# Second layer of a hybrid trunk: first attention pair ahead of the value projection, ends of the recurrent branch behind the first two pairs

## The chip, the cores and the metric

The kernel runs on one core of a Trainium2 chip. The metric is the device time of one execution in microseconds (us). The engines are PE (TensorE), DVE (VectorE), ACT (ScalarE), POOL (GpSimd) and SP (SyncE, here only a queue for transfers). Each works through its own list of instructions in order and waits on semaphores for the others.

## The reference, cut to what matters

A two-layer decoder trunk on 512 tokens of width 1024, all in float32. The second layer's mixer is what the change touches. One input projection gives xr, gr, q, k and v (512 columns each). xr and gr feed a recurrent branch, q, k and v a stick-breaking attention with 8 heads of 64. Their outputs, side by side, go through one output projection.

```python
# recurrent branch C
xc = conv_b + sum(conv_w[j] * xpad[:, j:j + S] for j in range(4))     # causal, width 4
r = sigmoid(xc @ wa + ba); i = sigmoid(xc @ wx + bx)                  # 8 diagonal blocks of 64
log_a = -8 * r * softplus(-lam)
a = exp(log_a); u = sqrt(-expm1(2 * log_a)) * (i * xc)
h[t] = a[t] * h[t-1] + u[t]                                           # a scan over time
yc = h * gelu(gr)
# attention D, per head
z = (q @ k.T) / 8                                                     # masked: k before q
s = where(mask, log_sigmoid(-z), 0)
w = where(mask, exp(log_sigmoid(z) + (suffix sum of s over keys) - s), 0)
yd = w @ v
```

## The kernel before

All activations are kept transposed, 128 features by 512 tokens. Every float32 matrix product of a projection is done as three products of a high and a low part (`mm3`): a tile of weights arrives by DMA in `ws` (one of 2 buffers), ACT copies it into its high part `wh`, DVE subtracts to get the low part `wl` (5 buffers each), and PE runs 8 x 3 matmuls of 128 x 512 into one PSUM bank (`proj`, 24 matmuls). The projections' banks have the tag "g", 2 banks in turn, so a projection waits until the bank of the last but one has been emptied.

In `layer1` the second layer's mixer runs in this order:

- `griffin(xr)`, the recurrent branch, with 4 tiles of 128 channels. The four xr tiles already lie in PSUM. Per tile j, ACT copies xr out (`xp`), DVE does the convolution in four operations (`xc`), PE multiplies by the two gate matrices (`pa`, `px`), ACT takes two sigmoids (`r`, `ig`) and a tanh of `r`, DVE multiplies `ig` by `xc`. Then four projections of gr follow, each with a gelu on ACT (`gt`). Then the ends: per tile 4 Ln and Exp operations on ACT and 10 operations on DVE, one of them the scan, and the high and low parts of the result (`yh`, `yl`).
- `values(S_VD)`, the value projection: four weight tiles, 4 x 24 matmuls.
- four times `sb_pair`, attention for two heads: Q and K projections (`qk_pair`, which splits the results into high and low parts on ACT and DVE); five tiles of scores `z` by PE, for each a copy on ACT, a minimum on DVE, Exp and Ln on ACT, a maximum on DVE, and a high and low part (`sh` on ACT, `sl` on DVE); then PE forms the cumulative sums (`cu`, for the five tiles in two banks in turn, 6, 8 and 8 matmuls for the last three), DVE adds each to its `z`, ACT takes the Exp, and PE multiplies by the values (`po`). The output projection of the recurrent branch (`out_rows`) stands behind the fourth pair in the text.

The order of instructions on each engine is not written out. A scheduler makes it when the program is built, from the order of the text, priorities (weights are taken early, by `self.hp`) and the buffers: a tile of a pool has a tag, the tags have fixed numbers of buffers, and a tile gets a buffer when it is first written. `act` has 16 buffers of 128 x 512 and is used in the whole kernel; `z`, `l`, `sh` and `sl` (6, 4, 5 and 5) belong to the second layer's mixer. Before, `xp` was an `act` tile, and `r`, `ig` and `gt` took the attention's tags `z`, `sh` and `sl`. What the scheduler sets is fixed at build time: at run time an engine only waits.

Of the kernel before, what the change touches and what calls it, by code (L numbers as in the profile page):

```python
# [7 lines left out]
F32 = mybir.dt.float32  # L8
# [3 lines left out]
AF = mybir.ActivationFunctionType  # L12
ALU = mybir.AluOpType
AX = mybir.AxisListType

P = 128
T = 512
# [36 lines left out]
class Trunk:  # L54
# [631 lines left out]
    def griffin(self, xr):  # L686
        nc, cp = self.nc, self.cp
# [28 lines left out]
        st = []  # L716
        for j in range(4):
            ps = xr[j]
            xp = self.sb.tile([P, T], F32, tag="act", bufs=16, name=self.nm("xp"))
            nc.scalar.copy(xp, ps)  # L720
            xc = self.t2k("xc", tag="l")
            w = lambda t: par[:, C_CW + 4 * j + t:C_CW + 4 * j + t + 1]
            nc.vector.tensor_scalar(xc, xp, w(3), par[:, C_CB + j:C_CB + j + 1], ALU.mult, ALU.add)
            for t in (1, 2, 3):
                nc.vector.scalar_tensor_tensor(xc[:, t:T], xp[:, 0:T - t], w(3 - t), xc[:, t:T], ALU.mult, ALU.add)
            pa = self.bank("sc", "pa")
            nc.tensor.matmul(pa, gw[0][:, j, :], xc, start=True, stop=True)
            px = self.bank("ho", "px")
            nc.tensor.matmul(px, gw[1][:, j, :], xc, start=True, stop=True)
            r = self.t2k("r", tag="z")  # L730
            A(r, pa, AF.Sigmoid, bias=par[:, C_BA + j:C_BA + j + 1])
            ig = self.t2k("ig", tag="sh")
            A(ig, px, AF.Sigmoid, bias=par[:, C_BX + j:C_BX + j + 1])
            A(r, r, AF.Tanh, scale=sp4[:, j:j + 1])
            nc.vector.tensor_tensor(ig, ig, xc, ALU.mult)
            st.append((r, ig))
        gts = []
        for j in range(4):
            ps = self.proj(S_GR + j)
            g = self.t2k("gt", tag="sl")  # L740
            A(g, ps, AF.Gelu_apprx_tanh)
            gi = self.newest()
            gts.append(g)
        with self.tc.issue_after(gi):
            nc.scalar.preload_act_table_set("natural_log_exp_and_others")
            pre = self.newest()
        ys = []
        for j in range(4):
            t, ix = st[j]
            dn = self.t2k("dn", tag="l")  # L750
            nc.vector.tensor_scalar(dn, t, 0.5, 0.5, ALU.mult, ALU.add)
            w = self.t2k("w", tag="l")
            with self.tc.issue_after(pre):
                A(w, dn, AF.Ln)
            A(w, w, AF.Exp, scale=-1.0)
            nc.vector.tensor_tensor(dn, dn, w, ALU.mult)
            nc.vector.tensor_scalar(dn, dn, -1.0, 2.0, ALU.mult, ALU.add)
            nc.vector.tensor_tensor(w, w, dn, ALU.mult)
            nc.vector.tensor_scalar(t, t, 1e-19, None, ALU.max)
            with self.tc.issue_after(pre):  # L760
                A(t, t, AF.Ln)
            A(t, t, AF.Exp, scale=0.5)
            nc.vector.tensor_tensor(ix, ix, t, ALU.mult)
            nc.vector.tensor_tensor(ix, ix, w, ALU.mult)
            nc.vector.tensor_scalar(w, w, 1.0, None, ALU.subtract)
            nc.vector.tensor_tensor_scan(ix, w, ix, 0.0, ALU.mult, ALU.add)
            nc.vector.tensor_tensor(ix, ix, gts[j], ALU.mult)
            yh, yl = self.act("yh"), self.act("yl")
            self.put(ix, yh, yl)
            ys.append((yh, yl))  # L770
        return ys


    def sb_pair(self, hp, v):
        nc = self.nc
        A = nc.scalar.activation
        q, k = self.qk_pair(S_QD + hp, S_KD + hp, self.kz)
        yh, yl = self.act("yh"), self.act("yl")
        po = self.bank("ho", "po")
# [28 lines left out]
        for ti, parts in enumerate(tiles):  # L808
            z = sp[parts]
            ps = self.bank(("pt", "po")[ti % 2], "cu")  # L810
            lo = [(self.none, sp[e, i], o + (i - j) * P, T - i * P) for e, j, o in parts for i in range(j + 1, NTB)]
            mms = [(self.ntri, sp[parts[0][:2]][:2] + (0,), 0, T)] + lo
            for n, (w, (sh, sl, oi), c, m) in enumerate(mms):
                for x in (sh, sl):
                    nc.tensor.matmul(ps[:, c:c + m], w, x[:, oi:oi + m], start=n == 0 and x is sh,  # L815
                                     stop=n == len(mms) - 1 and x is sl)
            nc.vector.tensor_tensor(z, z, ps, ALU.add)
            A(z, z, AF.Exp)
            ex = self.newest()

        at = {(e, j): (sp[parts], o) for parts in tiles for e, j, o in parts}
        for j in range(NTB):
            for e in range(2):
                h = 2 * hp + e
# [8 lines left out]
    def layer1(self, xr):  # L833
# [14 lines left out]
        self.hp = 1  # L848
# [124 lines left out]
```

## Time and profile before

| | us |
|---|---|
| median of 3 runs | 1266.29 (1264.41 to 1266.33) |
| the profiled execution, its time | 1266.0 |
| the profiled execution, its span | 1264.2 |
| the four xr projections end, first gate projection begins | 690.0 |
| value projection, its matmuls | 720 to 742 |
| first attention pair, its scores begin | 757.9 |

A row of the trace in order of time reads: start, duration, engine, line, operation, what is written and from what, its size, how many were merged, and in brackets the idle time before it and who ended it. A row of windows reads: from:to, length, busy us of PE, PEld (weight load), DVE, ACT and POOL with the number of instructions, then the granted clock of PE, the share of the DMA engines and GB/s. A matmul's duration is longer than the step from one matmul to the next, since they overlap. Line numbers are those of the kernel before; `L247` to `L249` are the three products of `mm3`, `L236` and `L237` make `wh` and `wl`.

### The profile page before, as it was taken

Reading aid. Unit: us, or ns where it says so; the run is one execution under the profiler, and the core shown is the slowest. Engines: PE = TensorE matmul, PEld = TensorE weight load, DVE = VectorE, ACT = ScalarE, POOL = GpSimd, SP = SyncE. Lnnn points to the kernel's source line nnn. Section 1 sums busy time; section 2 is a strip of 40 time slices with the busy share of each in tenths; the row PEclk is TensorE's granted clock in tenths of the full one; section 3 lists DMA queues with packets and bytes.
Section 4 is the critical chain, followed back from the end, with each engine's and each line's share of the span. In section 5 each row is a group of like instructions: output and inputs, shape, how many; then the busy total and the mean of one; then the engine's idle time right before and its main releaser. Section 6 shows DMA issues by size and latency. Waiting matters only on the chain.

```text
span 1264.2 us, 15623 instructions
## 1 busy us (share of the span) xinstructions
PE 1244.6 (98%) x6311; PEld 1006.6 (80%) x6311; DVE 690.3 (55%) x1039; ACT 485.3 (38%) x748; POOL 28.9 (2%) x51
## 2 busy tenths in 40 slices
PE   9999999999999999999999999999999999999997
PEld 6787777779888888888889776777988888888885
DVE  7538788769334333334377596786733333433437
ACT  7446557442322222222233757673322222222120
POOL 2000000000000000000000000000000000000001
PEclk9999999999999999999999998999999999999999
DMA  6332111133232233332324221102423332333321
GB/s 237 117 112 63 61 51 51 51 117 103 98 99 90 96 99 100 100 94 91 99 91 143 67 86 48 48 20 84 151 67 100 100 98 87 99 101 100 100 67 67
DMA packets 34984, 115.46 MB, mean 91 GB/s; under 512 B 4176, under 2 KB 5200, under 8 KB 34912
## 3 DMA queue, kind: packets, MB, share of 16 engines
q1 hardware_dynamic: 33504, 112.77, 28.3%
q10 hardware_dynamic: 1152, 1.66, 0.4%
q8 instruction: 49, 0.80, 0.2%
q14 instruction: 23, 0.19, 0.0%
q0 software_dynamic: 256, 0.03, 0.0%
HBM read 112.32 MB, written 2.10 MB: 91 GB/s over the span
## 4 chain that ended last, share of the span: by engine, by line
PE 89%; DVE 6%; DMA 2%; ACT 2%; issue 1%; SPq 0%; DVEq 0%; ACTq 0%
PE pf L248 13%; PE pf L247 13%; PE pf L249 13%; PE po L249 8%; PE po L247 8%; PE po L248 8%; PE pj L247 5%; PE pj L248 5%; PE pj L249 4%; DMA ws<-in_wst 2%; PE sc L493 1%; PE po L660 1%; PE cu L815 1%; PE pv L248 1%; PE pv L247 1%; PE tr L317 1%
## 5 line engine op out<-in xcount | busy, mean ns | idle before, releaser
L236 ACT CAST wh<-ws 128x1024 fp32r<-128x1024 f32 x177 | 186.4, 1053 | 525.8 <-PE pf L248 190.5
L237 DVE TENSOR_TENSOR wl<-ws,wh 128x1024 fp32r<-128x1024 f32 x177 | 216.5, 1223 | 308.8 <-ACT wh L236 302.9
L247 PE MATMUL pf<-xh,wh 128*128 128x512 f32 x640 | 249.0, 389 | 0.0
L248 PE MATMUL pf<-xl,wh 128*128 128x512 f32 x640 | 249.0, 389 | 0.0
L249 PE MATMUL pf<-xh,wl 128*128 128x512 f32 x640 | 249.0, 389 | 0.0
L249 PEld LDWEIGHTS pf<-xh,wl 128*128 128x128 f32 x640 | 120.1, 188 | 25.1
L247 PEld LDWEIGHTS pf<-xh,wh 128*128 128x128 f32 x640 | 120.1, 188 | 24.9
L248 PEld LDWEIGHTS pf<-xl,wh 128*128 128x128 f32 x640 | 120.1, 188 | 24.7
L247 PE MATMUL po<-wh,hh 128*128 128x512 f32 x352 | 137.4, 390 | 0.0
L249 PE MATMUL po<-wh,hl 128*128 128x512 f32 x352 | 137.1, 390 | 0.1
L248 PE MATMUL po<-wl,hh 128*128 128x512 f32 x352 | 137.0, 389 | 0.0
L415 DVE TENSOR_TENSOR s<-s,pf 128x512 f32<-128x512 f32 x44 | 30.3, 688 | 141.8 <-PE pf L249 140.4
L247 PE MATMUL pj<-xh,wh 128*128 128x512 f32 x256 | 104.6, 410 | 1.7 <-DVE qk L595 1.1
L249 PE MATMUL pj<-xh,wl 128*128 128x512 f32 x256 | 105.4, 412 | 0.0
L248 PE MATMUL pj<-xl,wh 128*128 128x512 f32 x256 | 103.6, 405 | 0.0
L249 PEld LDWEIGHTS po<-wh,hl 128*128 128x128 f32 x352 | 66.0, 188 | 14.5 <-DVE hl L243 0.7
L247 PEld LDWEIGHTS po<-wh,hh 128*128 128x128 f32 x352 | 66.1, 188 | 14.3 <-DVE xt L328 0.6
L248 PEld LDWEIGHTS po<-wl,hh 128*128 128x128 f32 x352 | 66.1, 188 | 13.5
L247 PEld LDWEIGHTS pj<-xh,wh 128*128 128x128 f32 x256 | 48.4, 190 | 14.2 <-issue 4.6
L249 PEld LDWEIGHTS pj<-xh,wl 128*128 128x128 f32 x256 | 48.4, 189 | 10.6 <-issue 2.3
L248 PEld LDWEIGHTS pj<-xl,wh 128*128 128x128 f32 x256 | 48.4, 189 | 10.1 <-issue 1.4
L328 DVE TENSOR_TENSOR xt<-xt,po 128x512 f32<-128x512 f32 x64 | 43.4, 685 | 14.8 <-PE po L249 14.7
(242 smaller groups left out, 1818.7 us busy)
## 6 DMA issues: line engine op xcount, KB each, us to landing
ws<-in_wst SPq DMA_DIRECT2D x189, 512.0 KB, 3.5
gb<-in_lnp SPq DMA_DIRECT2D x8, 512.0 KB, 4.8
ws<-in_wst SPq DMA_DIRECT2D x12, 256.0 KB, 5.2
xt<-in_xT SPq DMA_DIRECT2D x8, 256.0 KB, 4.9
xt<-in_x SPq DMA_DIRECT2D x1, 2048.0 KB, 7.8
out_y<-xt SPq DMA_DIRECT2D x4, 256.0 KB, 2.0
out_y<-xt ACTq DMA_DIRECT2D x4, 256.0 KB, 2.0
gw<-in_gw ACTq DMA_DIRECT2D x2, 256.0 KB, 3.2
```

Source lines behind the costliest of these rows:

```text
L236: nc.scalar.copy(hi, st)
L237: nc.vector.tensor_tensor(lo, st, hi.bitcast(F32), ALU.subtract)
L247: mm(ps, ah, bh, start=first, stop=False)
L248: mm(ps, ah, bl, start=False, stop=False)
L249: mm(ps, al, bh, start=False, stop=last)
L317: nc.tensor.transpose(ps[:, j * P:(j + 1) * P], y[:, h * T + j * P:h * T + (j + 1) * P], self.ident)
L328: self.nc.vector.tensor_tensor(y, y, ps, ALU.add)
L415: nc.vector.tensor_tensor(s, s, pb, ALU.mult)
L493: nc.tensor.matmul(ps[u:u + 64, c * 64:(c + 1) * 64], E[:, c * P + u:c * P + u + 64], rhs, start=True, stop=True)
L660: nc.tensor.matmul(po[d, c], v[j][:, h * 64:h * 64 + 64], pT[:, t0 + j * P:t0 + (j + 1) * P], start=j == 0, stop=j == i)
L815: nc.tensor.matmul(ps[:, c:c + m], w, x[:, oi:oi + m], start=n == 0 and x is sh, stop=n == len(mms) - 1 and x is sl)
```

## The change

Three edits. `r`, `ig` and `gt` become `act` tiles. The ends of the recurrent branch leave `griffin` for a function of their own, `griffin_end(j)`, unchanged in what they compute; two of them are placed after the weights of the first pair, two after those of the second. `sb_pair` is cut in two, `sb_weights` (Q, K, scores, cumulative sums, Exp) and `sb_values` (the product with the values), and the value projection is placed between the two for the first pair. The numbers of buffers stay.

```diff
-            r = self.t2k("r", tag="z")
+            r = self.sb.tile([P, T], F32, tag="act", bufs=16, name=self.nm("r"))
             A(r, pa, AF.Sigmoid, bias=par[:, C_BA + j:C_BA + j + 1])
-            ig = self.t2k("ig", tag="sh")
+            ig = self.sb.tile([P, T], F32, tag="act", bufs=16, name=self.nm("ig"))
             A(ig, px, AF.Sigmoid, bias=par[:, C_BX + j:C_BX + j + 1])
...
-            g = self.t2k("gt", tag="sl")
+            g = self.sb.tile([P, T], F32, tag="act", bufs=16, name=self.nm("gt"))
             A(g, ps, AF.Gelu_apprx_tanh)
...
-        ys = []
-        for j in range(4):
-            t, ix = st[j]
-            dn = self.t2k("dn", tag="l")
...
+        self.gr = [(r, ig, g) for (r, ig), g in zip(st, gts)]
+        self.pre = pre
+
+    def griffin_end(self, j):
+        nc = self.nc
+        A = nc.scalar.activation
+        t, ix, gt = self.gr[j]
+        dn = self.t2k("dn", tag="l")
...
-        yc = self.griffin(xr)
+        self.griffin(xr)
         self.hp = 600
-        v = self.values(S_VD)
-        self.hp = 600
-        yd = []
+        yc, yd = [], []
         for hp in range(4):
-            yd.append(self.sb_pair(hp, v))
+            at = self.sb_weights(hp)
+            if hp == 0:
+                v = self.values(S_VD)
+            if hp < 2:
+                yc += [self.griffin_end(2 * hp + i) for i in range(2)]
+            yd.append(self.sb_values(hp, v, *at))
             if hp == 3:
                 self.out_rows(yc, S_WO1)
```

How the instructions now stand, at the three places that the prediction speaks of. The first is ACT in the recurrent branch, from just after the copy of the first xr tile (`xp_5547`). `xp_5564`, `xp_5581` and `xp_5598` are the copies of the second to fourth xr tile, `r` and `ig` the two sigmoids (the second `r` of a tile is its tanh), `wh` a weight tile's high part. Before:

```order
L720 COPY xp_5564<-pj_5309 128x512
L720 COPY xp_5581<-pj_5310 128x512
L715 DMA gw_5543<-in_gw 128x512
L715 DMA gw_5544<-in_gw 128x512
L720 COPY xp_5598<-pj_5311 128x512
L731 ACT_TABLE_LOAD
L731 ACTIVATE r_5558<-pa_5554,par 128x512
L236 CAST wh_5840<-ws_5838 128x1024
L733 ACTIVATE ig_5560<-px_5556,par 128x512
L734 ACTIVATE r_5558<-r_5558,sp_65 128x512
L731 ACTIVATE r_5575<-pa_5571,par 128x512
L733 ACTIVATE ig_5577<-px_5573,par 128x512
```

Now:

```order
L715 DMA gw_5543<-in_gw 128x512
L715 DMA gw_5544<-in_gw 128x512
L731 ACT_TABLE_LOAD
L731 ACTIVATE r_5558<-pa_5554,par 128x512
L733 ACTIVATE ig_5560<-px_5556,par 128x512
L734 ACTIVATE r_5558<-r_5558,sp_65 128x512
L236 CAST wh_5789<-ws_5787 128x1024
L720 COPY xp_5564<-pj_5309 128x512
L731 ACTIVATE r_5575<-pa_5571,par 128x512
L734 ACTIVATE r_5575<-r_5575,sp_65 128x512
L733 ACTIVATE ig_5577<-px_5573,par 128x512
L720 COPY xp_5581<-pj_5310 128x512
```

The copy of tile j+1 now stands behind both sigmoids of tile j, where all four copies stood ahead of the first sigmoid; the weight tile ahead of the second copy is that of the first K projection, where it was one of the value projection.

The second place is PE at the end of the second gr projection (`pj_5654`) and the beginning of the third (`pj_5687`), with the gate products of tiles 2 and 3 (`pa_5588`, `px_5590`, `pa_5605`, `px_5607`):

```order
+L247 MATMUL pj_5654<-xh,wh_5650 128x512
+L248 MATMUL pj_5654<-xl,wh_5650 128x512
+L249 MATMUL pj_5654<-xh,wl_5651 128x512
+L727 MATMUL pa_5588<-xc_5583,gw_5543 128x512
+L729 MATMUL px_5590<-xc_5583,gw_5544 128x512
+L727 MATMUL pa_5605<-xc_5600,gw_5543 128x512
+L729 MATMUL px_5607<-xc_5600,gw_5544 128x512
 L247 MATMUL pj_5687<-xh,wh_5683 128x512
 L248 MATMUL pj_5687<-xl,wh_5683 128x512
```

The gate products of the last two tiles now stand together behind the whole second gr projection, with no projection's matmul between them; before, those of tile 2 stood after that projection's seventh matmul, those of tile 3 after its twenty-first, with fourteen matmuls between.

The third place is DVE in the second attention pair, where it adds the cumulative sums to the scores (`z` from `cu`), as PE's sums come. Before (`l` with `z` is the maximum, `sl` a low part, `qk` a part of the third pair's Q):

```order
L801 TENSOR_TENSOR l_6335<-l_6335,z_6334 128x512
L817 TENSOR_TENSOR z_6263<-z_6263,cu_6349 128x512
L817 TENSOR_TENSOR z_6281<-z_6281,cu_6358 128x512
L804 TENSOR_TENSOR sl_6346<-l_6335,sh_6345 128x512
L595 SCALAR_TENSOR_TENSOR qk_6409<-pj_6418,qk_6409 64x512
L817 TENSOR_TENSOR z_6299<-z_6299,cu_6367 128x512
L817 TENSOR_TENSOR z_6319<-z_6319,cu_6376 128x512
L817 TENSOR_TENSOR z_6334<-z_6334,cu_6387 128x512
```

Now (`dn`, `w`, `r` and `ig` are the recurrent ends of tiles 2 and 3; ahead of this piece stand a `wl` and two maxima):

```order
L819 TENSOR_TENSOR z_6220<-z_6220,cu_6306 128x512
L806 TENSOR_TENSOR sl_6288<-l_6277,sh_6287 128x512
L806 TENSOR_TENSOR sl_6303<-l_6292,sh_6302 128x512
L819 TENSOR_TENSOR z_6238<-z_6238,cu_6315 128x512
L819 TENSOR_TENSOR z_6256<-z_6256,cu_6324 128x512
L760 TENSOR_TENSOR dn_6355<-dn_6355,w_6357 128x512
L767 TENSOR_TENSOR ig_5594<-ig_5594,r_5592 128x512
L819 TENSOR_TENSOR z_6276<-z_6276,cu_6333 128x512
L761 TENSOR_SCALAR dn_6355<-dn_6355 128x512
L755 TENSOR_SCALAR dn_6375<-r_5609 128x512
L762 TENSOR_TENSOR w_6357<-w_6357,dn_6355 128x512
L819 TENSOR_TENSOR z_6291<-z_6291,cu_6344 128x512
```

The recurrent ends of tiles 2 and 3 now stand among the additions, and the last part of the third pair's Q, which frees the bank for the fourth pair's, has moved from ahead of the third addition to behind eight operations that follow the fifth.

More of the change, by code (lines that the diff above doesn't have):

```diff
@@ L746, in griffin @@
             pre = self.newest()
-        ys = []
-        for j in range(4):
-            t, ix = st[j]
-            dn = self.t2k("dn", tag="l")
[L751 to L770, printed above, removed]
@@ L775, in sb_pair, with sb_weights @@
+    def sb_weights(self, hp):
         nc = self.nc
@@ L777, in sb_pair @@
         q, k = self.qk_pair(S_QD + hp, S_KD + hp, self.kz)
-        yh, yl = self.act("yh"), self.act("yl")
-        po = self.bank("ho", "po")
         tiles = (((0, 3, 384), (0, 1, 0)), ((1, 3, 384), (1, 1, 0)), ((0, 2, 0), (1, 2, 256)), ((0, 0, 0),), ((1, 0, 0),))
@@ L819, in sb_pair, with sb_values @@
             ex = self.newest()
-        at = {(e, j): (sp[parts], o) for parts in tiles for e, j, o in parts}
+        return {(e, j): (sp[parts], o) for parts in tiles for e, j, o in parts}, ex
+    def sb_values(self, hp, v, at, ex):
+        nc = self.nc
+        yh, yl = self.act("yh"), self.act("yl")
+        po = self.bank("ho", "po")
         for j in range(NTB):
```

22 lines of the change are left out of this document (20 added, 2 removed).

## The prediction, made before the result was known

> **What bounds the kernel now.** I read the page first, then PE's rows in order of time from 676 to 870 us (the second layer's mixer), then ACT's and DVE's rows of the same stretch.
>
> ```profile
> PE 1244.6 (98%) x6311; PEld 1006.6 (80%) x6311; DVE 690.3 (55%) x1039; ACT 485.3 (38%) x748; POOL 28.9 (2%) x51
> ...
> PE 89%; DVE 6%; DMA 2%; ACT 2%; issue 1%; SPq 0%; DVEq 0%; ACTq 0%
> ```
>
> PE sets the end. The change leaves every matmul in place, so its worth is the difference in the time PE waits, or runs at a low clock. The first attention pair is the worst place of before:
>
> ```profile
> 753.69 0.47 PE L247 MATMUL pj<-xh,wh 128*128 128x512 f32 x1 [1.06 <-DVE qk L595]
> 757.90 0.33 PE L793 MATMUL z<-qk,qk 128*128 128x128 f32 x1 [1.02 <-DVE qk L600]
> 772.47 0.28 PE L815 MATMUL cu<-sl,none 128*128 128x128 f32 x1
> 775.13 0.80 PE L815 MATMUL cu<-sh,ntri 128*128 128x512 f32 x1 [2.39 <-DVE z L817]
> 781.49 0.28 PE L793 MATMUL z<-qk,qk 128*128 128x128 f32 x1
> ...
> 774.00:775.00 1.00, 0.00 (x0) 0.00 (x0) 1.00 (x2) 1.00 (x3) 0.00 (x0) 0.64 0.80 106
> 775.00:776.00 1.00, 0.87 (x2) 0.78 (x3) 1.00 (x3) 1.00 (x2) 0.00 (x0) 0.50 0.92 356
> 780.00:781.00 1.00, 1.00 (x4) 0.90 (x3) 0.96 (x2) 0.60 (x1) 0.00 (x0) 0.50 0.00 0
> 781.00:782.00 1.00, 1.00 (x10) 0.90 (x9) 0.31 (x1) 0.61 (x2) 0.00 (x0) 0.94 0.00 0
> ```
>
> Waits of 1.06, 1.02 and 2.39 us; and after the last one the granted clock (the last number but two in a window's row) is 0.50 until about 781.1, six us after PE had work again.
>
> **Gain in the first pair.** Its cumulative sums (6+8+8 matmuls) took 775.13 to 781.49, 6.36 us, at half clock. The second pair's same 22 took 4.02 us with a wait of 0.32 inside:
>
> ```profile
> 800.30 0.50 PE L815 MATMUL cu<-sh,ntri 128*128 128x512 f32 x1 [0.26 <-DVE z L817]
> 803.02 0.47 PE L815 MATMUL cu<-sh,ntri 128*128 128x512 f32 x1 [0.32 <-DVE z L817]
> 804.32 0.45 PE L247 MATMUL pj<-xh,wh 128*128 128x512 f32 x1
> ```
>
> So the low clock cost 6.36 - (4.02 - 0.32) = 2.7 us. With the waits that is 1.06 + 1.02 + 2.39 + 2.7 = 7.2, and about 0.4 for PE's restarts. The pair now has two blocks of the value projection as filler (48 matmuls, as many as the Q and K projections gave it), no recurrent end on DVE ahead of its K parts, and no weight tile among its exps: I leave it 0.4 us of waits. **-7.2 us.** Moving the projection's four weight transfers behind two others on SP's queue costs nothing: they have some 40 us before their use.
>
> **Loss in the recurrent branch.** The order in which ACT now stands (shown above) puts the copy xp of tile j+1 behind both sigmoids of tile j. The durations of that chain:
>
> ```profile
> 690.02 0.40 PE L247 MATMUL pj<-xh,wh 128*128 128x512 f32 x1
> 694.36 0.39 PE L248 MATMUL pj<-xl,wh 128*128 128x512 f32 x1
> 695.33 1.10 PE L727 MATMUL pa<-xc,gw 128*128 128x512 f32 x2 [0.59 <-PE pj L248]
> 698.52 1.02 PE L727 MATMUL pa<-xc,gw 128*128 128x512 f32 x2
> 699.62 0.40 PE L247 MATMUL pj<-xh,wh 128*128 128x512 f32 x1
> ...
> 690.22 0.82 ACTq L715 DMA_DIRECT2D gw<-in_gw  x2
> 696.47 0.69 ACT L731 ACTIVATE r<-pa,par 128x512 f32<-128x512 f32 x1 [3.50 <-PE pa L727]
> 698.03 1.05 ACT L236 CAST wh<-ws 128x1024 fp32r<-128x1024 f32 x1 [0.87 <-PE pj L248]
> 698.98 0.68 ACT L733 ACTIVATE ig<-px,par 128x512 f32<-128x512 f32 x1
> 699.57 0.71 ACT L734 ACTIVATE r<-r,sp 128x512 f32<-128x512 f32 x1
> 700.18 0.67 ACT L731 ACTIVATE r<-pa,par 128x512 f32<-128x512 f32 x1
> 710.54 1.28 ACT L741 ACT_TABLE_LOAD   x1
> 711.83 0.60 ACT L741 ACTIVATE gt<-pj 128x512 f32<-128x512 f32 x1
> ...
> DMA to landing us min/median/max: 2.8/3.2/3.7
> L723 DVE TENSOR_SCALAR xc<-xp,par x4: 535/680/898, 690.3 to 696.3; 128x512 f32<-128x512 f32 x4
> L725 DVE SCALAR_TENSOR_TENSOR xc<-xp,par,xc x12: 731/739/743, 691.9 to 701.8; 128x511 f32<-128x511 f32 x4, 128x510 f32<-128x510 f32 x4, 128x509 f32<-128x509 f32 x4
> 700.03 1.22 DVE L237 TENSOR_TENSOR wl<-ws,wh 128x1024 fp32r<-128x1024 f32 x1
> 701.16 0.68 DVE L735 TENSOR_TENSOR ig<-ig,xc 128x512 f32<-128x512 f32 x1
> ```
>
> A projection's matmul takes (694.36 - 690.02)/19 = 0.228 us, a gate product 699.62 - 698.52 - 0.23 = 0.87. On ACT a sigmoid or tanh takes 0.6 (0.7 where the next reads it), a wh 0.95; on DVE a convolution 0.6 + 3 x 0.74, a wl 1.15. Walked through in before's times:
>
> - *Tile 0.* Convolution and gw's landing at 693.4; pa and px to 695.3 (wait 0.6, as now). The first gate projection's last 11 matmuls end at 697.8.
> - *Tile 1.* ACT ends tile 0's tanh at 696.7 and meets wh, whose buffer is still read by that projection's 23rd matmul; as at 698.03 above, it waits, until 697.75. Behind it stands xp1, 698.7 to 699.3. The second gate projection needs the bank that xp1 empties: **wait 1.6.** It starts at 699.4. DVE does wl, then the convolution, to 702.9; 16 matmuls end at 703.0, no wait. pa, px and 8 matmuls end at 706.6.
> - *Tile 2.* r 704.1, tanh to 705.4, ig to 706.1, xp2 to 706.7; DVE multiplies ig, starts the convolution, does a wl in its middle, ends at 710.8. **Wait 4.2**, and PE has nothing else in its order.
> - *Tile 3.* After 4.2 idle us the clock is at half, as after 2.39 above. pa and px take 3.5 and end at 714.3; tanh, ig to 715.0, xp3 to 715.6, convolution to 718.6: **wait 4.3.** pa, px to 722.1.
> - *Gelu.* The third gate projection needs the bank of the first, emptied by a gelu that is now behind ig3 and a table load: 722.2 + 0.6 + 1.3 + 0.6 = 724.8, **wait 2.65.**
>
> The waits sum to 12.75, four gate products at half clock add 4 x 0.87 = 3.5, and tile 0 is unchanged: 16.2. Six us of half clock at the third projection, as after 775, lose another 3.0: **+19.2 us.** At full clock throughout it would be 1.6 + 4.2 + 4.8 + 2.9 = 13.5 (the third wait grows, since px ends earlier than r's chain). ACT saves two of five table loads here, 2.6 us, while it waits.
>
> **Loss in the second pair.** It now takes the filler and the neighbours that the first pair had: Q and K of the next pair, two weight tiles on ACT and DVE, and two recurrent ends instead of one.
>
> ```profile
> 773.19 1.29 DVE L801 TENSOR_TENSOR l<-l,z 128x512 f32<-128x512 f32 x2
> 774.39 0.68 DVE L817 TENSOR_TENSOR z<-z,cu 128x512 f32<-128x512 f32 x1
> 805.40 2.90 PE L826 MATMUL po<-z,v 128*64 128x512 f32 x16
> L818 ACT ACTIVATE z<-z x20: 621/631/634, 775.4 to 853.9; 128x512 f32<-128x512 f32 x20
> L766 DVE TENSOR_TENSOR_SCAN ig<-w,ig 128x512 f32<-128x512 f32 x4 | 4.9, 1223 | 0.1
> L757 DVE TENSOR_SCALAR dn<-dn 128x512 f32<-128x512 f32 x4 | 1.7, 422 | 0.0
> ```
>
> The wait of 2.39 came from a wl and two maxima ahead of the first addition; the same three stand there now. Its K parts are not late by the 1.02, so I bound it by 1.4 and 2.4 and take 1.9. Count on from the first addition's start. Two sl precede the second addition, which ends at 4 x 0.6 = 2.4 (two additions or maxima take 1.2 in the rows above); PE's first group of six (3.7 - 2 x 1.3 = 1.1 us, a group of eight being 804.32 - 803.02) ends at 0.6 + 1.1: it waits 0.8, and ends its two groups of eight at 5.1. DVE ends the third addition at 3.1; before the fifth stand five operations of the recurrent ends and the fourth addition, four of two inputs at 0.6 and two of one input at 0.34, 3.1 in all; addition and exp end at 3.1 + 3.1 + 0.7 + 0.7 = 7.6. po needs that exp and has no projection in front of it any more: 2.5. After po (2.9) the fourth Q projection waits for the last part of the third's Q, behind eight operations with a scan, about 5.3 us after the fifth addition: 1.75. Sum 6.95, less before's 0.26 + 0.32: **+6.4.** Whether the clock drops is open: the 2.5 exceeds the 2.39 that dropped it, but a slow po would run in time that PE waits anyhow. Between 0 and 2.7 I take 1.3: **+1.3.** The third and fourth pairs keep their order; between -2 and +2, taken as 0.
>
> **Sum.** 19.2 - 7.2 + 6.4 + 1.3 = +19.7, of which I take 19, since the branch's warm-up may be shorter. The profiled execution took 1266.0 us (span 1264.2 and 1.8 around it; the runs' median is 1266.29): **1285 us**.
>
> [...]
>
> **Rivals.**
> - *The waits are too short for the clock to matter* (chance 0.22): the branch costs 13.5 (never at half) to 16.2 (at half only between its waits), the second pair no clock: with -7.2 + 6.4 that is 1279 to 1281. For it: only one drop in 190 us of this stage. Against: 4.2 us idle is nearly twice the wait that dropped it.
> - *The second pair does not inherit* (0.15): ACT is faster than I think, the additions come in time: 19 - 6.4 - 1.3, so 1277. For it: the later pairs of before wait 0.3 at a time with similar neighbours.
> - *Both pairs of idle stretches halve the clock, the third pair is late too* (0.1): 1288 to 1292.
> - *Not slower* (0.05): the four waits of the branch vanish under the gate projections as they do now, where PE's rows between 690 and 708.9 show 0.6 us of waiting. Then -7.2 + 6.4 + 1.3, about 1266; it decides if the branch's waits stay under 3 us. Against it stands PE's order: between px2 and pa3 it has no other instruction, so a 3 us convolution is bare.
>
> **How the numbers follow.** The forecast has 0.48. The range takes in the second rival and part of the third: 1275 to 1291. A change under 0.2% (2.5 us) can't be told from none. Slower: 0.95; same 0.03, faster 0.02.
>
> **What would show it.** PE's rows around pa and px: waits of 1.6, 4.2, 4.3 and 2.7 us on DVE xc and ACT gt, a granted clock of 0.5 for some 15 us there, no wait over 1 us in the first pair, and in the second a wait over 1 us on DVE z ahead of its sums, of over 2 us ahead of po. If PE's waits at pa are under 1 us each, the walk is wrong, and the time falls to 1266 or below.

## The result, and the profile after

| | before | changed |
|---|---|---|
| median, us | 1266.19 | 1285.30 (1284.92 to 1286.24) |
| span of the profiled execution, us | 1264.2 | 1283.0 |
| ratio of the times, 95% interval | | 1.0154 (1.0138 to 1.0171) |

The changed kernel is 1.5% slower: 1285.3 us, where 1285.0 was forecast. Both medians are of four runs. The page of its profile answers to the one shown of before as follows (busy time by engine):

```profile
PE 1249.4 (97%) x6311; PEld 1005.8 (78%) x6311; DVE 690.3 (54%) x1039; ACT 482.3 (38%) x746; POOL 28.9 (2%) x51
```

The same number of matmuls keeps PE busy 4.8 us longer, while the span grew by 18.8: 14 us are idle time of PE, and most of the rest are matmuls at a low clock (PE was busy for 17.10 us at 0.50, in the three stretches whose windows stand below, and for 9.40 before, 3.41 from 245.22 and 5.99 from 774.29; half of the difference is 3.85 of the 4.8 us). Most of both stands in one place, the recurrent branch. These are PE's rows of the changed kernel in order of time there: its first instruction, its waits of over half a microsecond, the last of them ahead of the third gate projection (row 724.56), and a row of the fourth pair that is used further down.

```profile
688.91 0.40 PE L247 MATMUL pj<-xh,wh 128*128 128x512 f32 x1
...
698.43 0.50 PE L247 MATMUL pj<-xh,wh 128*128 128x512 f32 x1 [1.39 <-ACT xp L720]
709.96 2.05 PE L727 MATMUL pa<-xc,gw 128*128 128x512 f32 x2 [4.05 <-DVE xc L725]
718.12 2.04 PE L727 MATMUL pa<-xc,gw 128*128 128x512 f32 x2 [4.41 <-DVE xc L725]
724.56 0.50 PE L247 MATMUL pj<-xh,wh 128*128 128x512 f32 x1 [2.69 <-ACT gt L741]
...
869.18 0.47 PE L817 MATMUL cu<-sh,ntri 128*128 128x512 f32 x1 [0.16 <-DVE z L819]
```

From the first gate projection to the third, before took 690.02 to 708.92, 18.9 us; now it is 688.91 to 724.56, 35.65. Windows of the changed kernel over the same stretch, cut where the granted clock (the last number but two) changes:

```profile
708.82:722.47 13.65, 7.50 (x8) 2.35 (x8) 4.36 (x7) 4.54 (x7) 0.00 (x0) 0.50 0.13 40
...
725.88:729.29 3.41, 3.41 (x10) 2.67 (x9) 0.00 (x0) 0.00 (x0) 0.00 (x0) 0.50 0.00 0
```

PE has 7.50 us of work in the 13.65 us at half clock: the engines that it waits for (DVE 4.36, ACT 4.54) are not busy all the time either. It is a chain of single steps, each waiting for the one before.

ACT's rows show why. The copies `xp` of the second and third tile stand at 697.80 and 705.17, each behind the sigmoids of the tile ahead, which wait for PE (2.43 and 4.87):

```profile
693.68 0.69 ACT L731 ACTIVATE r<-pa,par 128x512 f32<-128x512 f32 x1 [2.43 <-PE pa L727]
...
697.80 0.58 ACT L720 COPY xp<-pj 128x512 f32<-128x512 f32 x1
703.25 0.69 ACT L731 ACTIVATE r<-pa,par 128x512 f32<-128x512 f32 x1 [4.87 <-PE pa L727]
...
705.17 0.57 ACT L720 COPY xp<-pj 128x512 f32<-128x512 f32 x1
```

The attention pairs: in the first pair the longest wait in PE's rows is now 0.16 us (at 766.59) and the clock stays at 1.00. These are the second pair's waits of over half a microsecond.

```profile
813.78 0.50 PE L817 MATMUL cu<-sh,ntri 128*128 128x512 f32 x1 [2.38 <-DVE z L819]
815.67 0.77 PE L817 MATMUL cu<-sh,ntri 128*128 128x512 f32 x1 [0.64 <-ACT r L766]
826.63 0.50 PE L247 MATMUL pj<-xh,wh 128*128 128x512 f32 x1 [2.22 <-DVE qk L595]
```

Windows of the same kernel, up to the fall of the clock and as long as it is low:

```profile
811.40:814.63 3.23, 0.85 (x6) 0.77 (x6) 3.23 (x6) 3.23 (x7) 0.00 (x0) 1.00 0.51 133
814.63:821.46 6.83, 6.19 (x21) 4.88 (x20) 5.48 (x11) 5.23 (x10) 0.00 (x0) 0.50 0.04 15
```

The waits and the low clock that left the first pair have come back in the second. Where PE waits 2.38 us at 813.78, DVE and ACT are busy without a pause (3.23 of 3.23 us). DVE's rows of that time show what stands ahead of the first addition to a `z`: a `wl` and two maxima (`l`).

```profile
810.70 1.23 DVE L237 TENSOR_TENSOR wl<-ws,wh 128x1024 fp32r<-128x1024 f32 x1 [0.25 <-ACT wh L236]
811.84 1.29 DVE L803 TENSOR_TENSOR l<-l,z 128x512 f32<-128x512 f32 x2
813.04 0.68 DVE L819 TENSOR_TENSOR z<-z,cu 128x512 f32<-128x512 f32 x1
```

### The profile page after: what moved, and what is told of

It is laid out like the page before. It is cut to its first block, busy times and chain, and to the rows that moved or that the text cites. A ratio compares the mean times of both kernels' runs of the same rounds, so it can differ in the third digit from the quotient of the medians.

```text
span 1283.0 us, 15623 instructions
## 1 busy us (share of the span) xinstructions
PE 1249.4 (97%) x6311; PEld 1005.8 (78%) x6311; DVE 690.3 (54%) x1039; ACT 482.3 (38%) x746; POOL 28.9 (2%) x51
## 4 chain that ended last, share of the span: by engine, by line
PE 89%; DVE 6%; ACT 3%; DMA 1%; issue 1%; SPq 0%; DVEq 0%; ACTq 0%
PE pf L248 12%; PE pf L247 12%; PE pf L249 12%; PE po L249 8%; PE po L247 8%; PE po L248 8%; PE pj L247 5%; PE pj L248 5%; PE pj L249 5%; PE sc L493 1%; PE pv L247 1%; PE pv L248 1%; PE pv L249 1%; PE po L660 1%; DMA ws<-in_wst 1%; PE tr L317 1%
```

## The experiments

Two theories were to be told apart. Mine: the recurrent branch pays nearly all of the loss, because `r`, `ig` and `gt` now take buffers from the same row as the copies `xp`. The rival: the new places of the value projection and of the recurrent ends pay it. Beyond that I wanted to know how much of the branch's loss is the low clock, what delays the second pair, and if a version of the change is worth having. Each kernel was compared with the kernel before on the same chip; the last column is (ratio - 1) x 1265 us, so it can differ by some tenths from a difference of medians. The intervals are about 1 to 2.6 us wide to each side.

| kernel | median, us | ratio to before, 95% | us over before |
|---|---|---|---|
| the change | 1285.3 | 1.0154 (1.0138 to 1.0171) | +19.5 |
| copies first | 1267.7 | 1.0021 (1.0012 to 1.0031) | +2.7 |
| tiles only | 1283.9 | 1.0144 (1.0127 to 1.0161) | +18.2 |
| copies from other buffers | 1269.1 | 1.0029 (1.0019 to 1.0039) | +3.7 |
| gaps kept busy | 1280.7 | 1.0119 (1.0104 to 1.0135) | +15.1 |
| values only | 1282.6 | 1.0141 (1.0127 to 1.0155) | +17.8 |
| all ends in the first pair | 1283.8 | 1.0139 (1.0118 to 1.0159) | +17.6 |
| copies first, all ends in the first pair | 1263.2 | 0.9981 (0.9972 to 0.9990) | -2.4 |
| copies first, ends 2 / 0 / 2 | 1269.6 | 1.0034 (1.0021 to 1.0048) | +4.3 |
| copies first, ends 2 / 1 / 1 | 1265.3 | 0.9998 (0.9988 to 1.0007) | -0.3 |
| the same, weights later | 1261.8 | 0.9976 (0.9967 to 0.9985) | -3.0 |
| the same, weights midway | 1265.2 | 0.9999 (0.9990 to 1.0008) | -0.1 |

### The copies first

```diff
-        st = []
-        for j in range(4):
-            ps = xr[j]
+        xps = []
+        for ps in xr:
             xp = self.sb.tile([P, T], F32, tag="act", bufs=16, name=self.nm("xp"))
             nc.scalar.copy(xp, ps)
+            xps.append(xp)
+        st = []
+        for j in range(4):
+            xp = xps[j]
```

> The changed kernel, with the four copies xp taken in a loop of their own ahead of the branch's loop over tiles, so that they get their buffers among the activations before any r or ig does. Nothing else differs. Theory (the shared buffers serialise the branch): the waits of 1.39, 4.05, 4.41 and 2.69 us and the half clock between them go, the branch takes 18.9 us again from the first gate projection to the third where it took 35.7, and the second pair stays as it is: about 1285.3 - 17 = 1268. Rival (most of the loss comes from the value projection's new place): at most 4 us are won, 1281 or more. Between them, 1272 to 1276, would mean that the waits went but the copies or r and ig bring a new one.

16.8 us of the 19.5 are gone. One window over the branch of this kernel:

```profile
688.20:707.20 19.00, 18.41 (x67) 11.93 (x66) 14.20 (x21) 12.52 (x18) 1.22 (x2) 1.00 0.19 56
```

PE is busy 18.41 of 19.0 us at a clock of 1.00: there is no room for a wait of more than the 0.6 that stood there before. The value projection and the ends are where the change put them, so they do not pay the 16.8. What is left, +2.7, is the balance of the first pair's gain and of what the later pairs lose. In this trace they lose more than in the change: their low clock lasts 6.82 us from 793.31, 3.42 from 806.97 and 3.42 from 827.45, where the pairs of the change have 6.83 in all. So the branch alone costs more than 16.8, by the rows of the change 16.75 up to the third gate projection and 1.7 of half clock behind it.

### The tiles only

In the kernel before, with the rest of it untouched:

```diff
-            r = self.t2k("r", tag="z")
+            r = self.sb.tile([P, T], F32, tag="act", bufs=16, name=self.nm("r"))
...
-            ig = self.t2k("ig", tag="sh")
+            ig = self.sb.tile([P, T], F32, tag="act", bufs=16, name=self.nm("ig"))
...
-            g = self.t2k("gt", tag="sl")
+            g = self.sb.tile([P, T], F32, tag="act", bufs=16, name=self.nm("gt"))
```

> The kernel before, with only r, ig and gt taken from the activations' buffers; the value projection, and the recurrent branch in one piece, stay where they were. Theory: the branch pays its whole loss here too, 1266.2 + 17 = 1283, with waits of about 1.4, 4, 4.4 and 2.7 us ahead of the gate products and the third gate projection. Rival (the wait needs the new places, too): 1266, with 0.6 us of waiting in the branch as before. Everything behind 745 us should look as before but for the shift.

The theory's number came out, +18.2 us for 17, with the branch's waits in PE's rows of this kernel:

```profile
699.65 0.50 PE L247 MATMUL pj<-xh,wh 128*128 128x512 f32 x1 [1.40 <-ACT xp L720]
711.19 2.05 PE L727 MATMUL pa<-xc,gw 128*128 128x512 f32 x2 [4.05 <-DVE xc L725]
719.77 2.05 PE L727 MATMUL pa<-xc,gw 128*128 128x512 f32 x2 [4.83 <-DVE xc L725]
726.15 0.50 PE L247 MATMUL pj<-xh,wh 128*128 128x512 f32 x1 [2.69 <-ACT gt L741]
```

So the new tiles are enough for the loss, and nothing else in the change is needed for it. Behind the branch it did not look quite as before: the first pair's sums have one more wait, of 0.81 us.

### The copies from other buffers

```diff
-            xp = self.sb.tile([P, T], F32, tag="act", bufs=16, name=self.nm("xp"))
+            xp = self.t2k("xp", tag="z")
```

> The changed kernel, order of the code untouched, but the four copies xp take their buffers from the scores' z tiles (free at that time) and no longer from the activations, where r, ig and gt now are. Theory (buffers of one kind are handed out in the order of the code, so xp of a tile stands behind r and ig of the one before): with a row of their own the copies are free again, the branch takes 18.9 us from the first gate projection to the third, and the time is that of the kernel with the copies first, 1285.3 - 16.5 = 1269 (1266 to 1271). Rival (the copies wait for their place in the code, or r and ig for lack of free buffers): the waits of 1.4, 4.0, 4.4 and 2.7 us stay, 1285.

+3.7 us, within the theory's range; a wait of 1.53 for the first copy, ahead of the first gate projection, is new. The text of the branch stands as in the change, and `r`, `ig` and `gt` are still `act` tiles; only the copies' row of buffers is another. A window of this kernel where the change has its low clock:

```profile
700.00:724.00 24.00, 24.00 (x98) 17.82 (x97) 8.01 (x9) 13.83 (x19) 0.00 (x0) 1.00 0.26 75
```

PE works 24.00 of 24 us. It is the shared row of buffers that orders the copies, not the place in the text; and not a lack of buffers either, as the kernel with the copies first draws as many from `act`.

### The gaps kept busy

```diff
             nc.tensor.matmul(px, gw[1][:, j, :], xc, start=True, stop=True)
+            if j:
+                dm = self.bank("pt", "dm")
+                for _ in range((4, 4, 2)[j - 1]):
+                    nc.tensor.matmul(dm, gw[0][:, j, :], xc, start=True, stop=True)
```

> The changed kernel with ten added gate products whose result nobody reads: four behind those of the second tile, four behind the third's, two behind the fourth's. They stand where PE has nothing else, and fill some 3.5, 3.5 and 1.7 us of its 4.05, 4.41 and 2.69 us of waiting, so that the clock should not fall. Theory (part of the branch's loss is the low clock): the chain through ACT and DVE stays, the granted clock stays 1.00 from 704 to 732, the four gate products take 0.87 and not 1.74 us each (of the 3.5 us so won the longer third wait takes 0.75 back) and the warm-up of 1.7 us goes: 1285.3 - 2.75 - 1.7 = 1281. Rival A (the chain alone sets the time, a slow PE works while ACT and DVE would have kept it waiting anyway): 1284 to 1286 at a clock of 1.00. Rival B (the added products are in the way): up to 1289.

This adds work: ten gate products that nobody reads. The time fell to 1280.7, 4.4 us under the change (19.5 - 15.1, each with about 2 us to either side). A window of this kernel:

```profile
704.00:732.00 28.00, 25.52 (x85) 15.59 (x84) 9.94 (x13) 11.24 (x17) 0.00 (x0) 1.00 0.12 37
```

And PE's third gate projection in it:

```profile
720.77 0.50 PE L247 MATMUL pj<-xh,wh 128*128 128x512 f32 x1 [1.44 <-ACT gt L745]
```

At a clock of 1.00 the third gate projection starts 3.79 us earlier (720.77 for 724.56), and the half clock behind it, worth 1.7 us, is gone. But not all of the 3.79 is the clock: 0.12 is an earlier start of the branch, and 1.01 is won between the second `pa` and the third, which took 7.77 us in the change (702.19 to 709.96) and take 6.76 here (702.07 to 708.83). The clock in the change fell only at 708.82, near the end of that step, when PE had been waiting there for some 2.9 us. What differs is DVE's order: in the change a `wl` stands in the middle of that convolution, here it does not.

```profile
707.15 1.22 DVE L237 TENSOR_TENSOR wl<-ws,wh 128x1024 fp32r<-128x1024 f32 x1
```

The other two steps (third `pa` to fourth, fourth to the projection) take 6.83 and 5.11 us here, 8.16 and 6.44 in the change: 2.66 us, which with the 1.7 behind them make 4.4 for the clock. The 1.01 does not show in the time. In this execution the later pairs have low clock for 3.41 us twice more than in the change (from 821.47 and 841.95), and from the third gate projection on the kernel takes as long as the change (558.5 and 558.4 us), although it is spared the 1.7. That the whole time fell by the same 4.4 is therefore luck. So of the branch's loss about 4.4 us are the clock, and the other 14 (16.75 and 1.7 of warm-up, less 4.4) the chain of waits; the prediction had 13.5 for a branch at full clock.

### The values only

In the changed kernel, with `ig` and `gt` put back in the same way:

```diff
-            r = self.sb.tile([P, T], F32, tag="act", bufs=16, name=self.nm("r"))
+            r = self.t2k("r", tag="z")
...
-        yc, yd = [], []
+        yc, yd = [self.griffin_end(i) for i in range(4)], []
...
-            if hp < 2:
-                yc += [self.griffin_end(2 * hp + i) for i in range(2)]
```

> The changed kernel's value projection behind the first pair's weights, but with r, ig and gt in the scores' buffers as before, and all four recurrent ends ahead of the first pair. It tells what moving the projection alone does. Theory (the projection's 96 matmuls were what PE did while DVE worked off the ends): the branch is free of waits, DVE does four ends and five wl, some 26 us from 720 on, ahead of the first Q's remainder, and PE, done with the first Q and K projections at 731, waits some 15 us for it and then 2 more at half clock; the first pair itself gains its 7.2, the second loses 2.4 and its clock: 1265.5 + 17 - 7.2 + 5 = 1280. Rival (the projection can be moved by itself for the gain of the first pair, less the second's loss): 1263 to 1265.

+17.8 us. The wait was a little longer than I thought. PE's row:

```profile
747.99 0.76 PE L247 MATMUL pv<-wh,xh 128*128 128x512 f32 x1 [18.42 <-DVE qk L595]
```

Three windows that follow the clock:

```profile
727.65:731.07 3.42, 1.91 (x9) 1.25 (x7) 3.42 (x6) 1.56 (x2) 0.00 (x0) 1.00 0.47 153
731.07:734.48 3.41, 0.00 (x0) 0.00 (x0) 3.41 (x7) 0.30 (x1) 0.00 (x0) 1.00 0.19 35
734.48:754.96 20.48, 6.71 (x19) 4.67 (x20) 18.96 (x31) 9.10 (x16) 0.00 (x0) 0.50 0.05 20
```

18.42 us of waiting for the first Q's remainder, for DVE works off the four ends ahead of it. In the kernel before, the value projection was what PE did meanwhile. So the three edits hang together: the projection can only move if the ends move, and the ends can only move if `r`, `ig` and `gt` lie in buffers that the attention doesn't need (that one by the code, it was not tried), and there the branch pays.

### All ends in the first pair, without and with the copies first

```diff
-            if hp < 2:
-                yc += [self.griffin_end(2 * hp + i) for i in range(2)]
+            if hp == 0:
+                yc += [self.griffin_end(i) for i in range(4)]
```

> The changed kernel, with all four ends of the recurrent branch behind the first pair's weights, none behind the second's. It tells what the two ends in the second pair cost. Theory (a wl and two maxima hold up the first addition, the ends only what comes later): the wait of 2.38 ahead of the sums and the half clock behind it stay, the wait of 2.22 us ahead of the fourth Q projection goes; the first pair keeps its gain since 48 matmuls of the value projection cover it: 1285.3 - 2.2 = 1283. Rival A (the ends are what delays the additions): the 2.38 and the low clock go too, 1285.3 - 7.5 = 1278. Rival B (four ends are too many for the first pair's filler, 22 us of DVE work against 22 us of the value projection): po of the first pair or the next K parts wait 2 to 6 us, 1286 to 1289.

> The changed kernel with both edits: the copies xp ahead of the loop, and all four ends behind the first pair's weights. If the two losses are independent, the differences add: 1285.3 - 17 - 2.2 = 1266 by the theories of the two single edits, 1261 if the ends are what delays the second pair's additions, 1270 if four ends are too many in the first pair. Under 1263.5 it would be faster than the kernel before.

The first came out near my number (1283.8), by another way than I wrote. PE's rows of the kernel without the copies first:

```profile
796.37 0.47 PE L247 MATMUL pj<-xh,wh 128*128 128x512 f32 x1 [2.40 <-DVE qk L595]
...
815.47 0.50 PE L817 MATMUL cu<-sh,ntri 128*128 128x512 f32 x1 [0.44 <-DVE z L819]
818.67 0.77 PE L817 MATMUL cu<-sh,ntri 128*128 128x512 f32 x1 [2.07 <-ACT sh L805]
```

The wait of 2.38 shrank to 0.44, as rival A had it, but a new one of 2.40 came up ahead of a projection, behind the ends, and one of 2.07 inside the sums. The expectation that the 2.38 stays was wrong: the scheduler, with other ends to place, also puts the `wl` elsewhere. It now starts at 815.34, right behind the first addition, ahead of the last maximum (817.24), and the wait of 2.07 is for what hangs on that maximum. With the copies first the same edit gives 1263.2, between the theory's number and rival A's, and 2.4 us faster than before. The two edits do not simply add: the ends in the first pair are worth 1.9 us without the copies first and 5.1 with them. The intervals of the first two ratios are 1.7 and 2.0 thousandths wide to each side, 2 to 2.6 us, so that the difference may be one of measurement alone. The traces have a candidate if it is more: with four ends in the first pair the low clock in the pairs grows from 6.83 to 10.24 us without the copies first, and falls from 13.66 to 6.82 with them. That this is the cause is not shown.

### Which ends behind which pair

On the kernel with the copies first, with ends 2 / 0 / 2 behind the first three pairs:

```diff
-            if hp < 2:
-                yc += [self.griffin_end(2 * hp + i) for i in range(2)]
+            yc += [self.griffin_end(i) for i in ((0, 1), (), (2, 3), ())[hp]]
```

The second kernel has 2 / 1 / 1, `((0, 1), (2,), (3,), ())`.

> The kernel with the copies first (1267.7 beside 1265.1 of the kernel before), but the recurrent ends 2 and 3 behind the third pair's weights and not the second's. Theory for the second pair: the wait of 2.38 us ahead of the sums stays, as it comes from a wl and two maxima, while the wait of 2.18 ahead of the fourth Q projection, 0.53 ahead of a po and the low clock behind these go, some 2.7 + 1.3: 1263.7. The third pair has 0.6 + 0.2 + 0.4 us of waits now; with two ends in it they may grow. Rival (the ends' cost moves with them to the third pair): 1267 to 1269. If the 2.38 goes too, the ends were in its cause: 1260.

> As the kernel with the copies first, but with ends 0 and 1 behind the first pair's weights, 2 behind the second's and 3 behind the third's. Theory: one end is about 8 operations and 5.5 us of DVE, so the wait of 2.18 ahead of the fourth Q projection shrinks to under 0.5 us, and the third pair takes the other end in its 0.6 us of slack: 1264, between the kernel before and the one with all four ends in the first pair, whose wait ahead of the third Q projection (2.67) and 2.08 in the second pair's sums do not come back. Rival (one end in each of two pairs costs a wait in each): 1267.

The kernel with two ends in the third pair was a miss, 1269.6 for 1263.7: the rival's time. PE's long waits in it:

```profile
795.58 0.50 PE L820 MATMUL cu<-sh,ntri 128*128 128x512 f32 x1 [2.38 <-DVE z L822]
833.79 0.80 PE L247 MATMUL po<-wh,yh 128*128 128x512 f32 x1 [4.98 <-DVE qk L595]
```

And in the kernel with 2 / 1 / 1:

```profile
795.21 0.50 PE L820 MATMUL cu<-sh,ntri 128*128 128x512 f32 x1 [2.39 <-DVE z L822]
830.92 0.50 PE L247 MATMUL po<-wh,yh 128*128 128x512 f32 x1 [1.02 <-DVE qk L595]
```

Two ends ahead of a Q's remainder cost PE 2.2 us in the second pair and 4.98 in the third, there with a clock of 0.50 for 10.24 us (from 831.50); one costs 1.02 in the third. For 2 / 1 / 1 I had expected 1264: the fourth Q projection's wait went, but the third pair's slack did not hold the other end, and the time was 1265.3. The wait ahead of the sums is 2.38 with no end in the second pair, 2.39 with one and 2.38 with two, each time behind a `wl` and two maxima: the ends have no part in it.

### The weights later

The lead given to a weight tile's high and low part in the attention, with ends 2 / 1 / 1:

```diff
         self.griffin(xr)
-        self.hp = 600
+        self.hp = 300
```

> As the last kernel (copies first; ends 0 and 1 behind the first pair's weights, 2 behind the second's, 3 behind the third's: 1265.3 beside 1265.5 of the kernel before), with one number changed: the lead given to the splitting of weight tiles (wh on ACT, wl on DVE) in the attention is 300 and no longer 600, so that in the second pair no wl stands ahead of the first addition to a z. Theory (the 2.38 us come from the wl and two maxima, and are there with two ends, one end or none in that pair): the wait falls under 0.5 us, and with it the half clock from 796 to 803 goes, which costs the 22 sums and what follows some 3: 1265.3 - 2 - 3 = 1260. Rival A (the maxima alone hold the addition up): the wait is 1.2 to 2.4, 1263 to 1266. Rival B (the weights now come late): PE waits for wl or wh ahead of a projection instead, 1265 to 1270.

The second kernel has 450 in this place.

> The same with a lead of 450: in the second pair a wl stands three places earlier, between the maxima, and the first two additions directly behind one another. Theory: the first addition is still delayed by part of that wl, a wait of 0.5 to 1.5 us, too short for the clock to fall: 1261 to 1263. If the wl's place decides nothing, 2.4 us and 1265.

With 300 no `wl` stands ahead of the first addition any more. PE's rows of that kernel around the second pair's sums:

```profile
794.55 0.47 PE L820 MATMUL cu<-sh,ntri 128*128 128x512 f32 x1 [0.17 <-DVE z L822]
796.59 0.47 PE L820 MATMUL cu<-sh,ntri 128*128 128x512 f32 x1 [0.58 <-ACT qk L592]
800.40 2.37 PE L836 MATMUL po<-z,v 128*64 128x512 f32 x14 [1.01 <-ACT z L823]
```

One window over its mixer:

```profile
700.00:870.00 170.00, 164.61 (x778) 124.37 (x777) 122.93 (x189) 110.63 (x184) 0.00 (x0) 1.00 0.20 62
```

The 2.39 is gone, the clock stays at 1.00 in the whole mixer, and the time is 1261.8, 0.24% under before (0.15 to 0.33). It is the lowest median here, though its interval overlaps that of the kernel with the copies first and all ends in the first pair. I had expected 1260; waits of 0.58 and 1.01 took some of the gain. This points to the `wl` as the cause, with two reserves: the lead moves other weight tiles too, and one of the two maxima also stands behind the first addition here (at 793.12, the addition at 792.52).

With 450 I was wrong: no gain at all. PE's rows around the same sums show a part of why:

```profile
792.03 0.50 PE L820 MATMUL cu<-sh,ntri 128*128 128x512 f32 x1 [0.18 <-DVE z L822]
795.76 0.47 PE L820 MATMUL cu<-sh,ntri 128*128 128x512 f32 x1 [1.16 <-ACT sh L808]
796.87 0.63 PE L820 MATMUL cu<-sl,ntri 128*128 128x512 f32 x1 [0.64 <-DVE sl L809]
```

The window behind them:

```profile
797.10:800.51 3.41, 3.41 (x10) 1.96 (x11) 2.72 (x6) 3.24 (x6) 0.00 (x0) 0.50 0.09 35
```

The first addition came in time, though a `wl` (at 788.50) and a maximum stand not far ahead of it. But two waits of 1.16 and 0.64 behind it, of a size that I took to be too short for the clock, were followed by 3.41 us at half clock. Their source in DVE's rows is a second `wl`, now between the second addition and the last maximum:

```profile
793.19 1.22 DVE L237 TENSOR_TENSOR wl<-ws,wh 128x1024 fp32r<-128x1024 f32 x1
```

Further on there are waits of 0.51 and 0.64 in the third pair's sums and of 1.18 at 834.42, and another 3.41 us of half clock from 834.65. Taken together: in the kernels looked at here in which at most one operation stands between a `wl` and the second pair's last maximum, a wait of over a microsecond follows, 2.38 or 2.39 ahead of the first addition, 2.07 or 1.16 inside the sums. In the kernel before, three operations stand between, and the wait is 0.26; the kernel with a lead of 300 has no `wl` there, and waits 0.17.

## Why the prediction was right, step by step

| step | predicted, us | measured, us |
|---|---|---|
| branch: waits ahead of projection, pa2, pa3, projection | 1.6, 4.2, 4.3, 2.65 | 1.39, 4.05, 4.41, 2.69 |
| branch, first to third gate projection | +16.2 | +16.75 |
| warm-up behind it | +3.0 | +1.7 |
| third gate projection to the fourth pair's sums, without the warm-up | +0.5 (-7.2 + 6.4 + 1.3) | +1.4 |
| from the branch's first matmul to the fourth pair's sums | +19.7, taken as 19 | +19.9 |

The last rows use one more row of PE in the kernel before, the fourth pair's wait that answers to 869.18 above:

```profile
850.40 0.47 PE L815 MATMUL cu<-sh,ntri 128*128 128x512 f32 x1 [0.17 <-DVE z L817]
```

Before, 690.02 to 850.40 is 160.38 us; now 688.91 to 869.18 is 180.27. The span grew by 1.1 less, since the branch began 1.1 us earlier in this execution (688.91 for 690.02). That has its origin ahead of the change; in the other kernels' traces the branch begins between 688.22 and 690.74.

That the forecast hit to 0.3 us is luck. Its mechanism held and its main term was 0.55 us too small, but the warm-up was 1.3 too large, the pairs 0.9 too small, the sum was rounded down by 0.7, and the earlier start took 1.1 off.

- *The branch.* The walk through ACT's order held to 0.2 us in each wait. It is also where the time is: the copies first alone takes 16.8 us away, the tiles alone bring 18.2.
- *The warm-up.* Mis-sized. I took six us of half clock, as after 775 in the kernel before. It was one stretch of 3.41 (725.88 to 729.29 above), a loss of 1.7. The low stretch of the kernel before, cut in the window below where its clock changes, is 6.83 us, twice as long. It began at 774.29, 1.55 us into the wait of 2.39 us, behind a stretch of 3.41 (from 770.88) in which PE was busy for 1.62.

```profile
774.29:781.12 6.83, 5.99 (x19) 5.29 (x20) 5.97 (x10) 3.72 (x8) 0.00 (x0) 0.50 0.26 76
```

- *First pair, -7.2.* Its waits of 1.06, 1.02 and 2.39 and its low clock are gone (0.16, clock 1.00). The size can't be read by itself, since the pair now has other work between its steps; the 0.4 for PE's restarts was my estimate, and no run shows it.
- *Second pair, +6.4 and the clock's +1.3.* The sum was about right, the items were not. The first addition kept PE for 2.38, not 1.9. The 2.5 ahead of `po` did not come: the sums ran at half clock for 6.83 us (814.63 to 821.46), and while they were slow the last exp was done. I had named that way out and taken the middle, 1.3, for the clock; it cost some 3 (half of 6.19 busy us). The fourth Q projection waited 2.22 for 1.75. 2.38 + 0.64 + 2.22 + 0.22 of waits and 3.1 of clock, less before's 0.58, are 8.0, against 7.7. The third pair, which the prediction took as 0, has one wait more than before, 0.63 us.
- *The cause of the first addition's delay.* The prediction gave a `wl` and two maxima, and left the ends out of it. The kernels with no, one or two ends in that pair bear out that the ends have no part; the ones with the `wl` in another place, or later, bear out the `wl`. The share of the two maxima was not told apart from it.
- *The rivals.* "The waits are too short for the clock to matter" fell: the clock was at 0.50 for 13.65 us in the branch, which by the rows cost 2.66 us, and 1.7 more behind it. "The second pair does not inherit" fell on rows 813.78 and 826.63. "Both pairs of idle stretches halve the clock, the third pair is late too" came true in part: the clock fell in the branch and in the second pair, and the third pair waited 0.63 more, but with 3.1 and 0.6 us that does not reach 1288. "Not slower" needed waits under 3 us at `pa`; they were 4.05 and 4.41.

## What to carry to other kernels

A row of buffers that is handed out in the order of the text orders the work of all who draw on it: before tiles are moved to a shared tag, look at who else takes from it, and let the one that must run ahead take its buffers first (or from a row of its own). Work that is moved away from under another engine's long stretch must be replaced by other work; here the value projection covered the recurrent ends, and moving it alone cost 18.42 us in one wait. And the length of a single wait did not tell here if the clock falls: after 1.16 and 0.64 us close together it went to 0.50 (797.10 in the kernel with 450), as in the wait of 2.39 us (774.29 before), while a wait of 2.22 us (826.63 in the change) left it at 1.00.

## What the runs showed of the hardware that I had not expected

In the mixer's traces the low clock came in whole steps of 3.41 us: one (in the change at 725.88, in the kernel with 450 at 797.10), two (6.83 in the change at 814.63), three (10.24 with two ends in the third pair), four (13.65 at 708.82), six (20.48 with the values only). The starts within one execution keep the same grid: in the change they lie 17.06 and 88.75 us apart, 5 and 26 steps of 3.413, in the kernel before 529.07 (245.22 to 774.29), 155 of them. A step of this grid is called a window below. The time from the start of a wait to the fall was not the same: 1.55 us into the wait of 2.39 in the kernel before (774.29), 2.91 us into that of 4.05 in the change (708.82), and in the change's second pair (814.63) 0.85 us after the wait of 2.38 had ended. Where the waits lie on the grid may therefore count; the kernel with the copies first points to it. Its third pair has nearly the waits of the change's third pair, yet its clock falls and the change's does not. Two of the waits in PE's rows of the copies-first kernel:

```profile
825.22 0.51 PE L820 MATMUL cu<-sh,none 128*128 128x256 f32 x2 [0.62 <-ACT sh L808]
...
827.29 0.67 PE L820 MATMUL cu<-sh,ntri 128*128 128x512 f32 x1 [0.44 <-DVE z L822]
```

Windows of the same kernel over them:

```profile
824.04:827.45 3.41, 2.12 (x12) 1.34 (x11) 3.36 (x7) 3.36 (x7) 0.00 (x0) 1.00 0.00 0
827.45:830.87 3.42, 3.42 (x12) 3.04 (x13) 2.96 (x5) 3.40 (x7) 0.00 (x0) 0.50 0.00 0
```

The same waits in the changed kernel:

```profile
843.74 0.51 PE L817 MATMUL cu<-sh,none 128*128 128x256 f32 x2 [0.63 <-ACT sh L805]
845.80 0.50 PE L817 MATMUL cu<-sh,ntri 128*128 128x512 f32 x1 [0.44 <-DVE z L819]
```

Windows of the changed kernel over them:

```profile
841.94:845.35 3.41, 2.56 (x14) 1.67 (x12) 3.18 (x6) 3.39 (x7) 0.00 (x0) 1.00 0.00 0
845.35:848.77 3.42, 2.64 (x16) 2.35 (x16) 3.36 (x6) 3.37 (x7) 0.00 (x0) 1.00 0.00 0
```

In the first the waits lie in one window (PE busy 2.12 of 3.41 us) and the next runs at half clock; in the second they are spread over two (2.56 and 2.64) and the clock stays at 1.00.

The spread between runs goes with the clock too. In the 21 runs of the kernel before on one chip, the two shortest (1263.26 and 1263.86) have a mean granted clock of 0.997, the two longest (1267.26 and 1267.46) one of 0.994. If a kernel's place on the grid differs from run to run, a gain or loss of one or two us by the low clock, as in the later pairs here, can belong to the execution and not to the kernel; with one trace per kernel this is not shown.

What makes the clock fall stays open. It fell behind a window with 2.12 us of work here, but in the kernel with the values only it stayed at 1.00 behind one of 1.91 (727.65 to 731.07) and fell only after an empty one, and in the change it stayed at 1.00 behind one of 1.65 as well (824.87 to 828.28, around the wait of 2.22). By the rows of this case the busy time alone does not decide it, and that the spread over two windows saved the change's third pair is likely, not shown.
